# Selector matmuls and split latent projections: row copies by DMA and plain float32 matmuls in a two-layer trunk

## The chip, the cores and the metric

The kernel runs on one core of a Trainium2 chip. The metric is the device time of one execution in microseconds (us). The kernel before takes 2700.78 us, the median of 3 runs (2699.51 to 2701.32). A core has five engines that run at the same time, each with its own queue in program order: TensorE (PE, matmuls; its weight loads are shown as PEld), VectorE (DVE), ScalarE (ACT), GpSimd (POOL) and SyncE (SP), which here issues all transfers. Matmul results land in PSUM (8 banks of 128 x 512 float32), everything else lives in SBUF or in DRAM.

## The reference

Two layers on x of 1024 tokens by 1024 features, float32. Each layer normalizes x, multiplies by `w_in` (1024 x 9180), runs three branches (sparse attention over latent keys, stick-breaking attention, mLSTM), gates and projects them, and adds the result to x. What the change touches:

```python
# sparse attention: keys and values of all 8 heads come from one latent of rank 128
q_abs = jnp.einsum('bshn,rhn->bshr', q_nope, w_uk)
kv_cat = jnp.concatenate([c_kv, k_rope], axis=-1)      # 16 rotary features beside the latent
logits = jnp.einsum('bthf,btkf->bthk', qb, kv_sel)
o = jnp.einsum('bshr,rhv->bshv', o_lat, w_uv)
# mLSTM, 4 heads of 128, per chunk of tokens
w_intra = jnp.exp(log_d - m_row[..., None])            # log_d = b_t - b_s + i_s
w_inter = jnp.exp(log_inter - m_row)
num = s @ v + w_inter[..., None] * (q @ c_mem)
c_mem = decay[..., None, None] * c_mem + sum_s(w_upd * k * v)
```

The kernel uses the equal form in which keys `w_uk.T @ c_kv` (48 features a head, 16 rotary ones beside them) and values are built once for each pair of heads, and mLSTM chunks of 128 tokens.

## The kernel before

`body` writes a log of operations for the five engines in a natural order. `Plan.run` then places them: it plays the log with a table of costs (`cost`), takes on each engine the ready operation of lowest priority number, gives out SBUF and PSUM slots, and so fixes one order for each engine, which `emit` writes down. A change of an operation or of a cost can therefore move instructions anywhere. One line of `emit` writes every instruction, so all rows of the profile have the line L533, and views are told apart by shapes, tiles and time.

Large products run in "float32r", a one-pass float32 with shortened inputs: each operand is split into a high and a low part, and `PASSES` adds three products (high-high, high-low, low-high). The attention phases and the mLSTM are interleaved with background work: the top-k search (`tick`) and the gates of the branches (`AHEAD`), whose matmuls the planner takes when nothing else is ready.

Names that the change touches:

- `selm(j)` is a column of `sel_ml` repeated 128 times. A matmul with it as stationary operand copies row j of the moving operand (high part plus low part) to all 128 partitions of PSUM. In the mLSTM the log decays `rr_` and the factors `wi` (32 rows, one for each chunk and head, of 128 tokens) are split, written to DRAM (`pkd`), read back as 16 rows (`pk`), and for each head `h` and half `th` of the tokens copied by `selm(h)` (decays) and `selm(4 + h)` (factors). A bfloat16 matmul of `identb` with `m_ml` adds the causal mask to the copied decays in PSUM. 16 more selector matmuls of 4 columns (8 a layer) fetch the chunks' last factors (`dec`).
- `dsa_k(pr)` builds the keys of a head pair: three float32r matmuls of 512 columns for each half, and a fourth with `sel_kr` that adds the rotary rows (`krs`) below both heads. `stack_k` copies the result into two tiles (high part of one head over low part of the other).
- `dsa_v(pr)` builds values: for each of 8 token blocks three float32r matmuls of 256 columns.
- Plain float32 matmuls are there already: in the mLSTM the scores (`cv`, 128 columns) and the products of 129 columns with `Wt`, `qs`, `kw`.

Of the kernel before, what the change touches and what calls it, by code (L numbers as in the profile page):

```python
# [126 lines left out]
def cost(eng, meth, args, kw, ins, outs):  # L127
    n = max(free_size(a) for a in ins + outs)
    if eng == "PE":
        if meth == "transpose":  # L130
            return 109.5
        c = free_size(ins[1])
        dt = ins[1].tensor.dtype
        if dt == F32:
            return 2 * max(c * 0.4445, 109.0) + 2.5
        return max(c * 0.4445, 107.0 if dt == F32R else 36.0) + 4.0
# [477 lines left out]
def body(log, tiles, caps, x_in, w_in, w_uk, w_uv, kvn, conv_w, ib, fb, mln, w_br, w_out, nrm, fnrm,  # L614
# [50 lines left out]
    sel_kr = const([128, 128], F32R, "sel_kr")  # L665
    zer = const([128, 48], F32, "zer")
    V.memset(zer, 0.0)
    for e in range(2):
        V.tensor_tensor(sel_kr[:, 64 * e:64 * e + 16], ident[:, 0:16], ident[:, 16:32], ALU.add)
        V.tensor_copy(sel_kr[:, 64 * e + 16:64 * e + 64], zer)  # L670
    sel_ml = const([128, 8], F32R, "sel_ml")
    for j in range(8):
        k = (j % 4) + 8 * (j // 4)
        V.tensor_tensor(sel_ml[:, j:j + 1], ident[:, k:k + 1], ident[:, k + 4:k + 5], ALU.add)
# [10 lines left out]

    def selm(j):
        return sel_ml[:, j:j + 1].to_broadcast([128, 128])
# [109 lines left out]
    for l in range(DEPTH):  # L797
# [317 lines left out]
        hl = half(F32R)  # L1115
        pkd = dram([4, 32, 128], F32R)
        for q, src in ((0, rr_), (2, wi)):
            split(src, hl[0:32, q * 128:q * 128 + 128], hl[0:32, q * 128 + 128:q * 128 + 256])
        for q in range(4):
            SY.dma_start(f(pkd[q]), f(hl[0:32, q * 128:q * 128 + 128]))  # L1120
        pk = []
        for th in range(2):
            k = half(F32R)
            pk.append(k)
            G.memset(f(k[:, :512]), 0.0)
            for q in range(4):
                SY.dma_start(f(k[4 * q:4 * q + 4, :512]).rearrange("h (c t) -> h c t", c=4),
                             f(pkd[q, 16 * th:16 * th + 16, :]).rearrange("(c h) t -> h c t", h=4))
# [5 lines left out]
        pd = pst("tr")  # L1134
        for h in range(4):
            for th in range(2):
                PE.matmul(pd[:, h * 8 + th * 4:h * 8 + th * 4 + 4], selm(4 + h),
                          pk[th][:, 127:512:128], start=True, stop=True)
        dec = small([128, 4, 8], name="dec", bufs=1)
# [615 lines left out]
```

## Time and profile before

| | |
|---|---|
| median of 3 runs | 2700.78 us |
| profiled execution | 2701.0 us |
| its span, first to last instruction | 2699.2 us |
| busy: PE, PEld | 2660.6 us (99%), 2245.6 us (83%) |
| busy: DVE, ACT, POOL | 1753.4 us (65%), 1484.8 us (55%), 1086.3 us (40%) |
| matmul records | 14802 |
| granted TensorE clock | 0.998 of full speed |

"Busy" of PE is the union of the records' durations. Matmuls overlap, so a record of 128x512 lasts 394 ns while the next one starts earlier; the rate is read from a stretch that holds one shape only: (busy time minus one duration) over (count minus one). The profile writes float32r and float32 both as "f32". The layers run one after the other; phases of a layer in order are the first projections and the scores of the top-k search (to about 100 us in layer 0), the mLSTM (to about 450 us), stick-breaking attention (to about 760 us), sparse attention (to about 1100 us), gates and output product (to about 1343 us). Layer 1 repeats this from there.

### The profile page before, as it was taken

What the parts mean: (1) busy time and instruction counts of PE and PEld (TensorE: products, weight loads), DVE (VectorE), ACT (ScalarE), POOL (GpSimd) and SP (SyncE); (2) the same over time, 40 slices, a digit from 0 to 9 for tenths busy, and PEclk for the clock granted to TensorE, in tenths of its full rate; (3) what the DMA queues carried; (4) which work ended last, traced back from release to release, by engine and by line L of the source; (5) the groups of instructions that cost most, each with busy time, mean ns of one, the idle gap of its engine ahead of it and who ended that gap; (6) DMA issues with size and microseconds to landing.
All of it is one profiled execution on the core that took longest, in us unless ns stands there. A gap on an engine that the chain in (4) does not pass through costs nothing.

```text
span 2699.2 us, 42025 instructions
## 1 busy us (share of the span) xinstructions
PE 2660.6 (99%) x14802; PEld 2245.6 (83%) x14802; DVE 1753.4 (65%) x4076; ACT 1484.8 (55%) x3004; POOL 1086.3 (40%) x1433
## 2 busy tenths in 40 slices
PE   8999999999999999999999999999999999999998
PEld 7888878888888888888898888888888888888886
DVE  5828789667586653426867287986676766634277
ACT  4637773545466857611446368735555677675023
POOL 4323334233253524444725143342342444244536
PEclk9999999999999999999999999999999999999999
DMA  4302112112122214664204021222121322256531
GB/s 132 99 16 65 54 55 72 51 55 80 36 88 68 78 55 141 224 222 152 76 25 120 14 79 52 63 67 59 36 75 44 96 59 71 62 179 230 180 117 63
DMA packets 234632, 236.86 MB, mean 88 GB/s; under 512 B 22250, under 2 KB 181300, under 8 KB 234420
## 3 DMA queue, kind: packets, MB, share of 16 engines
q1 hardware_dynamic: 234420, 234.17, 27.5%
q8 instruction: 117, 1.92, 0.3%
q14 instruction: 95, 0.78, 0.1%
HBM read 171.78 MB, written 62.32 MB: 87 GB/s over the span
## 4 chain that ended last, share of the span: by engine, by line
PE 51%; ACT 4%; DVE 2%; issue 1%; DMA 1%; POOL 0%; SPq 0%; DVEq 0%; ACTq 0%; POOLq 0%
PE t L533 51%; ACT t L533 3%; DVE t L533 2%; ACT s L533 1%; DMA t<-in_w_in_dram 1%; ACT L533 1%; POOL t L533 0%; DVE s L533 0%; SPq L533 0%; DMA d<-t 0%; DVEq L1751 0%; ACTq L533 0%; DVEq L533 0%; POOLq L533 0%
## 5 line engine op out<-in xcount | busy, mean ns | idle before, releaser
L533 PE MATMUL t<-t,t 128*128 128x512 f32 (+5 forms) x14094 | 2536.7, 342 | 27.8 <-DVE t L533 22.2
L533 PEld LDWEIGHTS t<-t,t 128*128 128x128 f32 x13950 | 2114.0, 183 | 397.6 <-DVE t L533 36.2
L533 POOL TENSOR_TENSOR t<-t,t 128x256 fp32r<-128x256 f32 (+3 forms) x946 | 754.3, 825 | 1074.3 <-ACT t L533 446.0
L533 DVE TENSOR_TENSOR t<-t,t 128x512 f32<-128x512 f32 (+15 forms) x1514 | 761.6, 534 | 592.7 <-ACT t L533 489.0
L533 ACT CAST t<-t 128x512 fp32r<-128x512 f32 (+6 forms) x1047 | 532.6, 551 | 473.3 <-PE t L533 240.7
L533 ACT ACTIVATE t<-t 128x512 f32<-128x512 f32 (+5 forms) x699 | 346.9, 592 | 266.4 <-PE t L533 196.5
L533 ACT ACTIVATE t<-t,t 128x768 bf16<-128x768 f32 (+7 forms) x343 | 273.6, 817 | 25.7 <-DVE t L533 19.6
L533 ACT COPY t<-t 64x256 f32<-64x256 f32 (+4 forms) x296 | 110.2, 380 | 257.2 <-PE t L533 254.9
L533 DVE TENSOR_TENSOR_SCAN t<-t 128x256 f32<-128x256 f32 (+10 forms) x144 | 209.3, 1463 | 7.1 <-ACT t L533 6.7
L533 DVE SCALAR_TENSOR_TENSOR t<-t,t,t 128x512 f32<-128x512 f32 (+7 forms) x220 | 166.7, 781 | 12.5 <-POOL t L533 5.3
L533 POOL TENSOR_SCALAR t<-t 64x512 fp32r<-64x512 f32 x128 | 85.2, 666 | 198.9 <-ACT t L533 145.3
L533 ACT ACT_TABLE_LOAD x114 | 146.3, 1283 | 23.7 <-PE t L533 14.5
L533 POOL TENSOR_SCALAR t<-t,t 128x256 f32<-128x256 f32 (+7 forms) x128 | 95.3, 753 | 134.1 <-DVE t L533 126.3
L533 DVE TENSOR_TENSOR s<-s,t 128x512 f32<-128x512 f32 (+1 forms) x93 | 67.4, 728 | 106.4 <-PE t L533 103.7
L533 DVE TENSOR_SCALAR_CACHE_REDUCE t<-t,t 128x512 bf16<-128x512 f32 (+5 forms) x169 | 125.7, 770 | 1.0
L533 PE MATMUL t<-s,t 128*128 128x512 f32 (+1 forms) x336 | 112.4, 386 | 0.0
L533 DVE CUSTOM_DVE_ANT_0 t<-t,t 128x512 f32<-128x512 f32 (+3 forms) x160 | 92.6, 592 | 21.3 <-PE t L533 18.7
L533 PEld LDWEIGHTS t<-s,t 128*128 128x128 f32 x336 | 62.0, 188 | 13.8
L533 DVE TENSOR_SCALAR t<-t 128x1 f32<-128x1 f32 (+5 forms) x324 | 58.0, 187 | 9.1 <-ACT t L533 6.5
L533 PE MATMUL t<-t,s 128*128 128x512 f32 (+1 forms) x200 | 63.3, 389 | 0.0
L533 DVE RECIPROCAL t<-t 128x1 f32<-128x1 f32 (+1 forms) x144 | 23.0, 163 | 61.2 <-ACT t L533 60.2
L533 DVE TENSOR_TENSOR t<-t 128x1 f32<-128x1 f32 (+9 forms) x234 | 54.4, 244 | 4.1 <-POOL t L533 1.6
(54 smaller groups left out, 823.4 us busy)
## 6 DMA issues: line engine op xcount, KB each, us to landing
t<-in_w_in_dram SPq DMA_DIRECT2D x192, 256.0 KB
d<-t SPq DMA_DIRECT2D x134, 256.0 KB
t<-d SPq DMA_DIRECT2D x119, 256.0 KB
t<-in_w_in_dram SPq DMA_DIRECT2D x44, 512.0 KB
s<-d SPq DMA_DIRECT2D x85, 256.0 KB
d<-t SPq DMA_DIRECT2D x130, 128.0 KB
t<-in_w_branch_dram SPq DMA_DIRECT2D x24, 512.0 KB
t<-in_x_dram SPq DMA_DIRECT2D x16, 512.0 KB
```

Source lines behind the costliest of these rows:

```text
L533: fn(*args, **kw)
```

## The change

The decays and factors of the mLSTM go to DRAM unsplit (`row_d`), and for each head and half one transfer with a partition step of zero copies the row to all 128 partitions of an SBUF tile (`row`). The mask is added to the decays by GpSimd. The chunk's last factor is read as a column of the same tile. In sparse attention the latent is kept unsplit, keys and values take one plain float32 matmul each, and the rotary rows are written into the finished key tiles by four small transfers for each half. The selector tiles go. The planner's price of a plain float32 matmul in `cost` changes.

```diff
         if dt == F32:
-            return 2 * max(c * 0.4445, 109.0) + 2.5
+            return 2 * max(c * 0.83 + 3.5, 109.0) + 2.5
...
-        hl = half(F32R)
-        pkd = dram([4, 32, 128], F32R)
-        for q, src in ((0, rr_), (2, wi)):
-            split(src, hl[0:32, q * 128:q * 128 + 128], hl[0:32, q * 128 + 128:q * 128 + 256])
-        for q in range(4):
-            SY.dma_start(f(pkd[q]), f(hl[0:32, q * 128:q * 128 + 128]))
-        pk = []
-        for th in range(2):
-            k = half(F32R)
-            pk.append(k)
-            G.memset(f(k[:, :512]), 0.0)
-            for q in range(4):
-                SY.dma_start(f(k[4 * q:4 * q + 4, :512]).rearrange("h (c t) -> h c t", c=4),
-                             f(pkd[q, 16 * th:16 * th + 16, :]).rearrange("(c h) t -> h c t", h=4))
+        row_d = dram([2, 32, 128])
+        for q, src in enumerate((rr_, wi)):
+            SY.dma_start(row_d[q], src)
+
+        def row(q, h, th):
+
+            r = half()
+            a = row_d[q, 16 * th + h:16 * th + h + 1, :]
+            SY.dma_start(r[:, :512].rearrange("p (c t) -> p c t", c=4),
+                         bass.AP(tensor=a.tensor, offset=a.offset, ap=[[0, 128], [512, 4], [1, 128]]))
+            return r
...
-        pd = pst("tr")
-        for h in range(4):
-            for th in range(2):
-                PE.matmul(pd[:, h * 8 + th * 4:h * 8 + th * 4 + 4], selm(4 + h),
-                          pk[th][:, 127:512:128], start=True, stop=True)
...
+            rows_ = []
+            for th in range(2):
+                r = row(0, h, th)
+                pool_tt(r, r, m_ml.rearrange("p a b -> p (a b)"), ALU.add, 512)
+                rows_.append((r, row(1, h, th)))
             tick(2)
             for th in range(2):
-                p = pst("lg")
-                PE.matmul(p, selm(h), pk[th][:, :512], start=True, stop=False)
-                PE.matmul(p, identb, m_ml.rearrange("p a b -> p (a b)"), start=False, stop=True)
+                rrow, wrow = rows_[th]
                 Wt = half()
                 for t in range(4):
                     c = th * 4 + t
-                    S.activation(Wt[:, t * 128:t * 128 + 128], p[:, t * 128:t * 128 + 128], AF.Exp,
+                    S.activation(Wt[:, t * 128:t * 128 + 128], rrow[:, t * 128:t * 128 + 128], AF.Exp,
                                  bias=mlc[:, 0, c, h:h + 1])
...
-                p = pst("lg")
-                PE.matmul(p, selm(4 + h), pk[th][:, :512], start=True, stop=True)
                 qs = half()
-                V.tensor_tensor(qs[:, :512], cv[0, th][:, :512], p, ALU.mult)
+                V.tensor_tensor(qs[:, :512], cv[0, th][:, :512], wrow[:, :512], ALU.mult)
...
-                            V.scalar_tensor_tensor(Cn, Cst, dec[:, h, c:c + 1], p[:, :129], ALU.mult, ALU.add)
+                            V.scalar_tensor_tensor(Cn, Cst, wrow[:, t * 128 + 127:t * 128 + 128], p[:, :129],
+                                                   ALU.mult, ALU.add)
...
         for th in range(2):
             c = half()
             SY.dma_start(c[:, :512], ckvT_d[:, th * 512:th * 512 + 512])
-            hi, lo = pair(F32R)
-            split(c[:, :512], hi, lo)
...
-            k = half(F32R)
-            G.memset(f(k[:, :512]), 0.0)
-            for q in range(2):
-                SY.dma_start(f(k[16 * q:16 * q + 16, :512]), f(kr_d[q, :, th * 512:th * 512 + 512]))
-            krs.append(k)
+            ck.append(c)
...
-            uw = half(F32R)
-            S.copy(uw[:, 0:128], us[:, :128])
-            G.tensor_tensor(uw[:, 128:256], us[:, :128], f(uw[:, 0:128]), ALU.subtract)
             r = dict(k=[], q=[None, None], z=[None, None])
             for th in range(2):
                 p = pst("mm")
-                for i, (a, b) in enumerate(PASSES):
-                    PE.matmul(p, uw[:, 128 * a:128 * a + 128], ck[b][th][:, :512], start=(i == 0), stop=False)
-                PE.matmul(p, sel_kr, krs[th][:, :512], start=False, stop=True)
-                r["k"].append(stack_k(p))
+                PE.matmul(p, us[:, :128], ck[th][:, :512], start=True, stop=True)
+                k = stack_k(p)
+                for e in range(2):
+                    for q in range(2):
+                        o = 64 * (e ^ q)
+                        SY.dma_start(f(k[e][o:o + 16, :512]), f(kr_d[q, :, th * 512:th * 512 + 512]))
+                r["k"].append(k)
...
-                    for i, (a, b) in enumerate(PASSES):
-                        PE.matmul(p[:, t * 256:t * 256 + 256],
-                                  ck[b][sb // 4][:, (sb % 4) * 128:(sb % 4) * 128 + 128],
-                                  uw[:, 256 * a:256 * a + 256], start=(i == 0), stop=(i == 2))
+                    PE.matmul(p[:, t * 256:t * 256 + 256], ck[sb // 4][:, (sb % 4) * 128:(sb % 4) * 128 + 128],
+                              us[:, :256], start=True, stop=True)
```

What the planner makes of it is shown in three places. The rows below are an engine's instructions in order: operation, output tile, inputs (for a matmul the moving and then the stationary one), shape; buffers have numbers of their own in each kernel. The first place is PE at the first head of the mLSTM, layer 0, before. `t_2286` takes `selm(0)` (`t_114`, moving `pk` as `t_1377`) and the mask, `t_2302` takes `selm(4)`.

```order
L533 MATMUL t_2270<-t_93,t_1708 128x128 x4
L533 MATMUL t_2277<-t_93,t_1755 128x128 x4
L533 MATMUL t_2286<-t_1377,t_114 128x512
L533 LDWEIGHTS t_97
L533 MATMUL t_2286<-t_103,t_97 128x512
L533 MATMUL t_2292<-t_1607,t_1708 128x128 x4
L533 MATMUL t_2302<-t_1377,t_114 128x512
L533 MATMUL t_2304<-t_1790,t_2283 128x129
L533 MATMUL t_2308<-t_1790,t_2283 128x129
```

The same place now, from the same transposes (`t_2240`, `t_2248`) on:

```order
L533 MATMUL t_2240<-t_92,t_1670 128x128 x4
L533 MATMUL t_2248<-t_92,t_1742 128x128 x4
L533 MATMUL t_2258<-t_1578,t_1670 128x128 x4
L533 MATMUL t_2267<-t_1771,t_2256 128x129
L533 MATMUL t_2269<-t_1771,t_2256 128x129
L533 MATMUL t_2273<-t_1833,t_2256 128x129
L533 MATMUL t_2278<-t_1833,t_2256 128x129
L533 MATMUL t_1432<-t_218,t_1282 128x512
L533 MATMUL t_2283<-t_1630,t_1742 128x128 x3
L533 MATMUL t_2291<-t_1771,s_1934 128x129
```

The three 512-column matmuls are gone, and four products with `kw` (`t_2256`) have come forward to stand between the scores (`t_2258`) and the first product with `Wt` (`s_1934`). The second place is PE at the first keys and values of sparse attention, layer 0, before: `t_9193` and `t_9202` are the keys of the two halves (the last matmul of each with `sel_kr`, `t_87`), the four tiles of 256 columns are the values.

```order
L533 MATMUL t_9193<-t_8369,t_8826 128x512 x3
L533 MATMUL t_9193<-t_8315,t_87 128x512
L533 MATMUL t_9202<-t_8406,t_8826 128x512 x3
L533 MATMUL t_9202<-t_8317,t_87 128x512
L533 MATMUL t_9213<-t_8871,t_8369 128x256 x6
L533 MATMUL t_9224<-t_8871,t_8369 128x256 x6
L533 MATMUL t_9234<-t_8871,t_8406 128x256 x6
L533 MATMUL t_9245<-t_8871,t_8406 128x256 x6
L533 MATMUL t_9257<-t_93,t_8844 128x128 x4
```

The same place now; `t_9138` is a key tile made from `t_9129`, and the last row shown is the first that reads it.

```order
L533 MATMUL t_9129<-t_8297,t_8672 128x512
L533 MATMUL t_9135<-t_8303,t_8672 128x512
L533 MATMUL t_9142<-t_8712,t_8297 128x256 x2
L533 MATMUL t_9152<-t_8712,t_8297 128x256 x2
L533 MATMUL t_9160<-t_8712,t_8303 128x256 x2
L533 MATMUL t_9170<-t_8712,t_8303 128x256 x2
L533 MATMUL t_9179<-t_92,t_8828 128x128 x4
L533 MATMUL t_9187<-t_212,t_8869 128x512
...
L533 MATMUL t_9187<-t_259,t_8918 128x512
L533 MATMUL t_9235<-t_9138,t_9197 128x128
```

Eight matmuls of 512 columns have become two, and 24 of 256 have become eight; behind them stand, as before, four transposes and the 24 matmuls of a gate (`t_9187`, two of which are shown) until the first logits. The third place is SP, where transfers are issued, at the start of the mLSTM of layer 0, before (`d_1586` is `pkd`, `t_1377` and `t_1379` are `pk`):

```order
L533 DMA d_1586<-t_1580 32x128 x3
L533 DMA t_1605<-in_w_in_dram 128x4x256
L533 DMA d_1586<-t_1580 32x128
L533 DMA t_1377<-d_1586 4x4x128 x3
L533 DMA t_1379<-d_1586 4x4x128 x3
L533 DMA t_1377<-d_1586 4x4x128
L533 DMA t_1379<-d_1586 4x4x128
L533 DMA t_1649<-in_w_in_dram 128x4x256
```

and now (`d_1560` is `row_d`; the tiles it is read into are the rows of head 0, and the two `s` tiles at the end those of head 1):

```order
L533 DMA d_1560<-t_1548 32x128 x2
L533 DMA t_1638<-in_w_in_dram 128x4x256
L533 DMA t_1823<-d_1560 128x4x128
L533 DMA t_1829<-d_1560 128x4x128
L533 DMA t_1838<-d_1560 128x4x128
L533 DMA s_1859<-d_1560 128x4x128
L533 DMA t_1968<-in_w_in_dram 128x4x128
L533 DMA t_1979<-in_w_in_dram 128x4x128
L533 DMA t_1968<-in_w_in_dram 128x4x128
L533 DMA t_1979<-in_w_in_dram 128x4x128
L533 DMA s_2182<-d_1560 128x4x128 x2
L533 DMA s_2205<-d_1560 128x4x128 x2
```

Eight small reads at the start have become four transfers of 256 KB for each head, which stand between the weight loads.

## Rows read from the trace of the kernel before

**Rows 1.** The page: span, busy time by engine, granted TensorE clock in 40 slices.
```profile
span 2699.2 us, 42025 instructions
PE 2660.6 (99%) x14802; PEld 2245.6 (83%) x14802; DVE 1753.4 (65%) x4076; ACT 1484.8 (55%) x3004; POOL 1086.3 (40%) x1433
PEclk9999999999999999999999999999999999999999
```

**Rows 2.** Waits of PE, whole span: us in total, times, longest.
```profile
PE t L533 <- DVE t L533: 22.2, 20, 7.9
PE t L533 <- ACT t L533: 1.9, 6, 0.4
PE t L533 <- POOL t L533: 1.0, 4, 0.5
```

**Rows 3.** Groups by shape on PE, 1495 to 1538 us: xcount | busy, mean ns.
```profile
L533 PE MATMUL t<-t,t 128*128 128x512 f32 x187 | 43.5, 394 | 0.0
```

**Rows 4.** The same on PE, 1772 to 1792 us.
```profile
L533 PE MATMUL t<-t,t 128*128 128x256 f32 x172 | 20.4, 280 | 0.0
```

**Rows 5.** The same on PE, 211.2 to 212.35 us (a run of plain float32 matmuls).
```profile
L533 PE MATMUL t<-t,t 128*128 128x129 f32 x11 | 1.4, 275 | 0.0
```

**Rows 6.** The same on PE, 128.58 to 129.24 us (the decays' selector matmuls).
```profile
L533 PE MATMUL t<-t,t 128*128 128x4 f32 x7 | 0.8, 239 | 0.0
```

**Rows 7.** Groups by shape on PE, whole span.
```profile
L533 PE MATMUL t<-t,t 128*128 128x129 f32 x344 | 56.6, 283 | 6.5 <-DVE t L533 5.9
L533 PE MATMUL t<-t,t 128*128 128x512 bf16 x16 | 6.2, 390 | 0.0
L533 PE MATMUL t<-t,t 128*128 128x4 f32 x16 | 2.0, 230 | 0.0
L533 PE MATMUL t<-t,s 128*128 128x129 f32 x8 | 1.4, 274 | 0.0
```

**Rows 8.** Groups by shape on POOL, whole span: additions of 256 columns.
```profile
L533 POOL TENSOR_TENSOR t<-t,t 128x256 f32<-128x256 f32 x32 | 22.9, 738 | 134.3 <-DVE t L533 134.3
```

**Rows 9.** Busy time of each engine in the mLSTM and sparse attention phases.
```profile
core 0: us, PE busy (x) PEld busy (x) DVE busy (x) ACT busy (x) POOL busy (x), PEclk, DMA share, GB/s
195.00:450.00 255.00, 249.72 (x1410) 214.71 (x1409) 212.12 (x562) 172.21 (x335) 94.79 (x126) 0.99 0.20 59
1480.00:1760.00 280.00, 277.56 (x1502) 234.13 (x1500) 194.15 (x518) 183.19 (x350) 97.59 (x138) 1.00 0.18 53
760.00:1100.00 340.00, 337.68 (x2013) 285.85 (x2012) 203.14 (x583) 232.68 (x480) 144.61 (x209) 1.00 0.30 92
2050.00:2440.00 390.00, 385.78 (x2305) 326.34 (x2304) 252.20 (x672) 277.83 (x579) 156.29 (x225) 1.00 0.29 88
```

**Rows 10.** The page: DMA queue, packets, MB, share of 16 engines' span.
```profile
q1 hardware_dynamic: 234420, 234.17, 27.5%
```

**Rows 11.** Timeline of SP, 121 to 127 us: start, us, xcount.
```profile
121.81 3.71 SPq L533 DMA_DIRECT2D t<-d  x8
125.57 1.49 SPq L533 DMA_DIRECT2D t<-in_w_in_dram  x3
```

**Rows 12.** Timeline around PE's longest wait after the start: start, us, [idle before].
```profile
346.48 1.88 DVE L533 TENSOR_TENSOR t<-t,t 128x512 f32<-128x512 f32 x3
347.23 1.17 PE L533 MATMUL t<-t,t 128*128 128x129 f32 x3 [3.95 <-DVE t L533]
```

**Rows 13.** The chain that ended last, 2096 to 2106 us: start, us, what.
```profile
2097.01 0.34 SPq L533
...
2097.44 6.23 DMA t<-in_w_in_dram
...
2103.70 1.05 ACT t L533
...
2105.17 0.43 DVE t L533
```

**Rows 14.** Groups by shape on ACT and DVE, whole span: the copies of `stack_k` and `stack_q`.
```profile
L533 ACT CAST t<-t 64x512 fp32r<-64x512 f32 x128 | 74.9, 587 | 60.8 <-PE t L533 36.8 <-DVE t L533 22.2
L533 DVE TENSOR_TENSOR t<-t,t 64x512 fp32r<-64x512 f32 x128 | 92.2, 721 | 55.8 <-ACT t L533 52.4 <-POOL t L533 1.6
```

More of the change, by code (lines that the diff above doesn't have):

```diff
@@ L664, in body @@
     V.memset(neghalf, -0.5)
[L665 to L674, printed above, removed]
     tk_thr = const([128, 6], F32, "tk_thr")
@@ L684, in body @@
             V.memset(tk_sign[:, i:i + 1], -0x80000000)
-    def selm(j):
-        return sel_ml[:, j:j + 1].to_broadcast([128, 128])
     def bcast(ap, n):
@@ L1133, in body @@
         V.tensor_copy(mlc.rearrange("p q c h -> p (q c h)"), p[:, 0:96])
-        pd = pst("tr")
-        for h in range(4):
-            for th in range(2):
-                PE.matmul(pd[:, h * 8 + th * 4:h * 8 + th * 4 + 4], selm(4 + h),
-                          pk[th][:, 127:512:128], start=True, stop=True)
-        dec = small([128, 4, 8], name="dec", bufs=1)
-        V.tensor_copy(dec, pd[:, 0:32].rearrange("p (h c) -> p h c", h=4))
         SCL = 128.0 ** -0.5
@@ L1432, in body @@
             return
-        ckh, ckl = [], []
-        krs = []
+        ck = []
         for th in range(2):
@@ L1439, in body @@
             SY.dma_start(c[:, :512], ckvT_d[:, th * 512:th * 512 + 512])
-            hi, lo = pair(F32R)
-            split(c[:, :512], hi, lo)
-            ckh.append(hi)
-            ckl.append(lo)
-            k = half(F32R)
-            G.memset(f(k[:, :512]), 0.0)
-            for q in range(2):
-                SY.dma_start(f(k[16 * q:16 * q + 16, :512]), f(kr_d[q, :, th * 512:th * 512 + 512]))
-            krs.append(k)
-        ck = (ckh, ckl)
+            ck.append(c)
         def dsa_q(gq):
@@ L1484, in dsa_v @@
             SY.dma_start(us[:, :256], w_uv[l, :, 2 * pr:2 * pr + 4, :].rearrange("r h c -> r (h c)"))
-            uw = half(F32R)
-            S.copy(uw[:, 0:256], us[:, :256])
-            G.tensor_tensor(uw[:, 256:512], us[:, :256], f(uw[:, 0:256]), ALU.subtract)
             vs = [[], []]
```

## The prediction

> **What bounds the kernel now.** I read the page first: PE is busy for 2660.6 of 2699.2 us, the other engines for 65% or less, and the granted clock stands at full speed in every slice [rows 1]. The waits of PE come next: 22.2, 1.9 and 1.0 us for DVE, ACT and POOL, 25.1 together, of which the longest, 7.9, is the start [rows 2]. So beyond the start only some 17 us of the span are waits of PE that a new order could remove, and nearly everything else is matmuls one behind the other. The third view is the rate of each shape. In stretches with one shape only, 512 columns of float32r take (43.5 - 0.394)/186 = 0.232 us each [rows 3], 256 columns (20.4 - 0.28)/171 = 0.118 us [rows 4]. A plain float32 matmul leaves two records: the mLSTM has 22 products of 129 columns for each of 8 heads, 176 in all, and the trace holds 344 + 8 = 352 [rows 7]. A record of these takes (1.4 - 0.275)/10 = 0.112 us [rows 5]. In all four phases that the change touches PE is busy for 98 to 99% of the stretch [rows 9]. A matmul taken away there is therefore time taken away, unless a new wait fills the place.
>
> **The mLSTM's matmuls.** For each of 2 layers, 4 heads and 2 halves three matmuls of 512 columns go: two selectors and the mask. The mask's is bfloat16; its 390 ns [rows 7] are those of a float32r one (394), so I price it alike. 16 x 3 x 0.232 = 11.1 us go. The decays' 16 selector matmuls of 4 columns [rows 7] take (0.8 - 0.239)/6 = 0.09 us, some 0.1 [rows 6]: 1.6 us go. Together -12.7 us, all on PE.
>
> **The latent products.** Keys: 2 layers x 4 pairs x 2 halves = 16 times, four matmuls of 512 columns (4 x 0.232 = 0.927) become one plain one. Values: 2 layers x 2 calls x 8 blocks = 32 times, three of 256 (3 x 0.118 = 0.353) become one plain one. The trace has no plain matmul wider than 129 columns, so I bound it. At least, each of its two records costs as much as a float32r matmul of that width: 0.464 and 0.235 us; then the keys give 16 x 0.463 = 7.4 and the values 32 x 0.118 = 3.8 us. At most, each record costs two of them: 0.927 and 0.471; then the keys give nothing and the values lose 32 x 0.118 = 3.8 us. The nearest row is the plain product of 129 columns: 0.112/129 = 0.868 ns a column and record, nearly twice the 0.232/512 = 0.453 of float32r. At this narrow width 0.112 could also be a floor that has nothing to do with columns (the selector matmuls of 4 columns take almost as much [rows 6]), which is why the lower end stays. I take the row: 512 columns cost 2 x 0.444 = 0.889, 256 cost 0.444. Keys: 16 x (0.889 - 0.927) = -0.6 us. Values: 32 x (0.444 - 0.353) = +2.9 us. So this half of the change loses 2.3 us by my reading, with ends at -11.2 and +3.8.
>
> The Trainium skill has a rule that speaks against this half: the page "FP8 and Floating Point Precision", section "TensorE Precision Notes", says that a true float32 product takes four passes through the array. By it a plain matmul costs four float32r ones, 0.927 and 0.471, the keys are even, the values lose 3.8 us, and the whole sum would be -8.9 us. The two records for each product fit two passes in each; no row here shows a width at which passes could be counted.
>
> **What the copies cost elsewhere.** The rows' mask goes to POOL: 16 rows x 2 pieces x 0.738 [rows 8] = 23.6 us of POOL, which is busy for 95 of 255 and 98 of 280 us in the mLSTM [rows 9]. That hides it as long as it comes before the exponentials. 32 transfers of 256 KB are 8.4 MB; 234 MB take 27.5% of 16 engines' span [rows 10], so these take 1.0% more, in phases where the engines are used to 0.18 and 0.20. SP issues a read in 3.71/8 = 0.46 and a weight load of the rows' shape in about 0.50 us [rows 11]: 32 x 0.50 + 64 x 0.46 for the rotary rows, less 0.46 for each of some 32 small ones that go, +31 us of a queue that issues some 930 transfers in 2700 us. ACT reads the decays from SBUF where it read PSUM, the same 128-column exponentials; the `qs` product on DVE has both inputs in SBUF. Splits on ACT, DVE and POOL go. None of this is on PE; I put it at nothing, covered by PE's own stream, and at up to the rivals' prices if that cover is gone.
>
> **The added waits.** A key tile is read only when its rotary rows have landed. The tightest place is the first pair, where the order of the change has behind the first key matmul one more key matmul (0.89), eight of 256 columns (3.6), four transposes (0.1 each, by the floor above) and the gate's 24 matmuls (5.6 us) before the first logits: 10.5 us. In this time come two copies on ACT and two on DVE, 2 x (0.587 + 0.721) = 2.6 us [rows 14], four issues, 1.9, and a landing, at most the 6.2 that weight loads took in a busy stretch [rows 13]: 10.7 us at worst. I take no wait there. Behind the rotary transfers on SP stand mask and weight loads and the stores of finished heads, which is a rival's matter below.
>
> **The sum.** -12.7 - 0.6 + 2.9 = -10.4 us. The profiled execution took 2701.0 (span 2699.2 and 1.8 around it), 0.2 above the median of 2700.78. 2701.0 - 10.4 = 2690.6, against the median 2690.4; I say 2690. For comparison: a measurement tells a change from none at about 0.2%, 5.4 us here.
>
> **Rival 1: plain matmuls are no slower than one float32r record each.** Then the sum is -12.7 - 11.2 = -23.9 us, 2677. For it speaks only that the 0.112 us of [rows 5] could be a floor; against it, weakly since both are read from short runs, that a selector of 4 columns, with less to stream, comes out below 0.112 [rows 6].
>
> **Rival 2: the new order eats the gain.** The planner places everything anew, and small misjudgements come out elsewhere. Before, PE's waits beyond the start sum to 17 us, one of them 3.95 us behind a late DVE product [rows 12]. Two or three more of that size give back 8 to 12 us: 2698 to 2702, no change. Against it: the same 17 us can also shrink, the mLSTM has one PSUM product and its wait less in every half, and the order around the three places shown is otherwise the one of before. If the waits shrink by half instead, 2682.
>
> **Rival 3: SP's queue holds the weights up, and the kernel is slower.** SP issues in order. At 2097 us a store waited for ACT; two weight loads behind it landed 6.23 us later, and through ACT (1.05) and DVE (0.43) their lateness reached PE [rows 13]. The change puts eight transfers that wait for `stack_k` into this queue at each of 8 pairs, and four row transfers that wait for free tiles at each of 8 heads. If each of these 16 places makes PE wait for about 2 us, the kernel is at -10.4 + 32 = +22 us, 2722. It decides from (10.4 + 5.4)/16 = 1.0 us for each place. Against it: all of PE's waits beyond the start are 17 us, this chain's among them, and the places lie far apart: by [rows 9] a head of the mLSTM spans some 255/4 = 64 us and a pair some 340/4 = 85, in which weights can be loaded ahead.
>
> **Rival 4: POOL's additions hold DVE in the mLSTM.** DVE is busy there for 212 of 255 and 194 of 280 us [rows 9], PE's waits are nearly all for DVE [rows 2], and additions of 23.6 us could delay DVE by as much, in the worst case all of it passed on: -10.4 + 23.6 = +13, 2714. The point is a delay on PE of 15.8 us, two thirds of the additions' whole time; since DVE has 43 and 86 us to spare there, I hold this unlikely. The Trainium skill, "SBUF — State Buffer", section "SBUF: two separate sides", says that a GpSimd operation and a VectorE one with both inputs in SBUF lock each other out for a whole instruction. The rows here show no instruction of either kind alone and beside the other, so the rule stands unproved in this case.
>
> **Chances.** The forecast, 2684 to 2697: 0.62. Rival 1: 0.07. The waits shrink, below 2684: 0.04. Rival 2, within 5.4 us of before: 0.15. Rival 3: 0.08. Rival 4: 0.04. Faster by over 0.2%: 0.62 + 0.07 + 0.04, less 0.01 for the forecast's upper edge: 0.72; within: 0.15 + 0.01 = 0.16; slower: 0.12. The range goes from rival 1's 2677 to 2703, just over rival 2's waits; outside it lie rivals 3 and 4 and little else.
>
> **What will show it.** In the profile after, PE's records should be 14802 - 48 - 16 - 16 x (4 - 2) - 32 x (3 - 2) = 14674, its busy time some 10 us less, with the waits of PE near 25 us. In runs of the key and value products a record should take about 0.44 us at 512 columns and 0.22 at 256: 0.23 and 0.12 would mean rival 1. The mLSTM stretches should be shorter by about 6 us in each layer, sparse attention longer by about 1. PE waits for DVE above 35 us in the mLSTM would speak for rival 4, waits of ACT for weight loads with PE behind them for rival 3, and scattered new ones for rival 2. The forecast is wrong if the records are gone and the span is not about 10 us shorter.

## The result

The changed kernel takes 2676.78 us (median of 4 runs, 2673.4 to 2679.29) against 2701.05 for the kernel before beside it: a ratio of 0.9912, interval 0.99 to 0.9923, 24 us faster. The forecast was 2690 with a range of 2677 to 2703, so the direction was right, the gain was more than twice the 10.4 us of the sum, and the time lies just below the range.

The page after, first lines, against [rows 1]:

```profile
span 2675.3 us, 41890 instructions
PE 2641.5 (99%) x14674; PEld 2234.8 (84%) x14674; DVE 1745.4 (65%) x4053; ACT 1480.8 (55%) x2986; POOL 1110.6 (42%) x1445
```

The 14674 records are those forecast. PE's busy time fell by 19.1 us and the span by 23.9, where both were to fall by about 10. PE's waits after (who is waited for: us, times, longest), against [rows 2]:

```profile
PE t L533 <- DVE t L533: 16.3, 14, 8.0
PE t L533 <- ACT t L533: 3.7, 3, 2.6
PE t L533 <- POOL t L533: 2.4, 6, 0.8
```

They sum to 22.4 us, 2.7 less than before. So the view of waits shows little of the 14 us that came on top of the forecast; most of it is inside PE's busy time, because a record lasts longer than the step to the next one.

To see it, I priced every record in program order at its shape's rate in a pure run (us for each record: float32r of 512, 256, 384, 220, 128 columns 0.232, 0.118, 0.176, 0.111, 0.061; plain of 512, 256 and 128 or 129 columns 0.429, 0.216, 0.1115; transposes 0.109; bfloat16 of 512 and 128 columns 0.232 and 0.039; the few others 0.11). Their sum I call **work**. The time from the first to the last start of a record, less the work, I call **slack**: the waits of the view and all small delays together, worked out by me from the records and shown by no view. From first to last start it is 2680.2 us before and 2657.0 after. Work is 2591.0 and 2579.5 (-11.5), slack 89.3 and 77.7 (-11.6). The work came out about as forecast; the slack had been put at no change.

Where the slack went, by the phase of the record that came late, both layers together: mLSTM 15.1 to 7.9, gates in the background 7.1 to 2.3, sparse attention 31.4 to 31.1, stick-breaking attention 24.5 to 24.1, first projections 3.3 to 4.6, the start 7.8 and 7.9.

**The plain products.** The weight loads of PE in the changed kernel, 2132.5 to 2138.1 us, show their rate (start, us, xcount, [idle before]); the loads before 2134.54 belong to keys of 512 columns, 16 of the group of 17 behind them to values of 256:

```profile
2133.26 0.19 PEld L533 LDWEIGHTS t<-t,t 128*128 128x128 f32 x1 [0.24 <-issue]
2133.68 0.19 PEld L533 LDWEIGHTS t<-t,t 128*128 128x128 f32 x1 [0.24 <-issue]
2134.11 0.19 PEld L533 LDWEIGHTS t<-t,t 128*128 128x128 f32 x1 [0.24 <-issue]
2134.54 3.60 PEld L533 LDWEIGHTS t<-t,t 128*128 128x128 f32 x17 [0.24 <-issue]
```

A record of 512 columns takes 0.43 us (2134.54 - 2134.11), one of 256 about (3.60 - 0.19)/16 = 0.213, a little low because the last load of the group is a shorter one; the matmuls' own starts give 0.429 and 0.216. Forecast were 0.444 and 0.222; rival 1 needed 0.23 and 0.12.

**The mLSTM's products of 129 columns.** Groups by shape on PE in the changed kernel (xcount | busy, mean ns | idle before them), against the 6.5 us idle in [rows 7]:

```profile
L533 PE MATMUL t<-t,t 128*128 128x129 f32 x264 | 43.9, 277 | 2.0 <-DVE t L533 1.9
L533 PE MATMUL t<-t,s 128*128 128x129 f32 x88 | 14.4, 274 | 0.0
```

The wait of 3.95 us [rows 12] has gone.

### The profile page after: what moved, and what is told of

It is laid out like the page before. It is cut to its first block, busy times and chain, and to the rows that moved or that the text cites. A ratio compares the mean times of both kernels' runs of the same rounds, so it can differ in the third digit from the quotient of the medians.

```text
span 2675.3 us, 41890 instructions
## 1 busy us (share of the span) xinstructions
PE 2641.5 (99%) x14674; PEld 2234.8 (84%) x14674; DVE 1745.4 (65%) x4053; ACT 1480.8 (55%) x2986; POOL 1110.6 (42%) x1445
## 4 chain that ended last, share of the span: by engine, by line
PE 89%; ACT 4%; DVE 3%; issue 2%; DMA 1%; POOL 1%; SPq 0%; POOLq 0%; ACTq 0%; DVEq 0%
PE t L533 89%; ACT t L533 3%; DVE t L533 3%; DMA t<-in_w_in_dram 1%; ACT L533 1%; POOL t L533 1%; DMA t<-in_x_dram 0%; ACT s L533 0%; DMA d<-t 0%; SPq L533 0%; DVE s L533 0%; POOLq L1716 0%; ACTq L533 0%; POOLq L533 0%; DVEq L533 0%
## 5 line engine op out<-in xcount | busy, mean ns | idle before, releaser
L533 PE MATMUL t<-t,t 128*128 128x512 f32 (+6 forms) x13826 | 2503.9, 343 | 23.9 <-DVE t L533 16.3
L533 POOL TENSOR_TENSOR t<-t,t 128x256 fp32r<-128x256 f32 (+4 forms) x956 | 772.0, 836 | 1016.9 <-ACT t L533 433.5
L533 DVE TENSOR_TENSOR t<-t,t 128x256 fp32r<-128x256 f32 (+12 forms) x1492 | 744.9, 528 | 588.0 <-ACT t L533 479.7
L533 ACT CAST t<-t 128x512 fp32r<-128x512 f32 (+5 forms) x1030 | 525.9, 552 | 489.9 <-PE t L533 260.8
L533 ACT ACTIVATE t<-t 128x512 f32<-128x512 f32 (+5 forms) x700 | 347.6, 587 | 262.2 <-PE t L533 200.5
L533 ACT ACTIVATE t<-t,t 128x1024 bf16<-128x1024 f32 (+9 forms) x320 | 288.8, 906 | 36.0 <-DVE t L533 30.0
L533 DVE SCALAR_TENSOR_TENSOR t<-t,t,t 128x512 f32<-128x512 f32 (+9 forms) x202 | 162.2, 826 | 10.4 <-POOL t L533 6.3
L533 ACT ACT_TABLE_LOAD x116 | 148.8, 1283 | 14.7 <-PE t L533 10.5
L533 POOL TENSOR_SCALAR t<-t,t 128x128 f32<-128x128 f32 (+7 forms) x128 | 95.7, 756 | 131.1 <-DVE t L533 126.0
L533 POOL TENSOR_TENSOR t<-s,s 128x256 fp32r<-128x256 f32 x52 | 53.4, 1052 | 53.8 <-issue 28.7
L533 DVE TENSOR_SCALAR t<-t 128x1 f32<-128x1 f32 (+6 forms) x324 | 59.7, 193 | 9.1 <-ACT t L533 6.8
L533 PE MATMUL t<-s,s 128*128 128x512 f32 x192 | 63.0, 394 | 0.0
```

Source lines behind the costliest of these rows:

```text
L533: fn(*args, **kw)
```

## The experiments

All ratios stand against the kernel before, run beside them on the same chip; it took 2699.36 to 2701.05 us there. Work, slack and the mLSTM's part of the slack are worked out from the trace of each, and each trace is one order of the operations. In the traces of `before_x1`, `before_x3`, `lat_x1`, `lat_x3`, `kr_only`, `plain_only` and `before_junk` 8 matmul records are missing; they are priced with the rest:

| kernel | time, us | ratio, interval | work | slack | mLSTM |
|---|---|---|---|---|---|
| before | 2700.78 | | 2591.0 | 89.3 | 15.1 |
| before_cost | 2701.62 | 1.0003 (0.9994-1.0013) | 2591.0 | 90.4 | 16.5 |
| before_x1 | 2707.93 | 1.0031 (1.0019-1.0042) | 2591.0 | 95.9 | 20.6 |
| before_x3 | 2707.02 | 1.0026 (1.0015-1.0037) | 2591.0 | 92.9 | 19.1 |
| ml_only | 2679.41 | 0.9925 (0.9909-0.9942) | 2578.1 | 78.8 | 7.0 |
| lat_only | 2691.65 | 0.997 (0.9958-0.9982) | 2592.4 | 77.6 | 16.1 |
| lat_x1 | 2689.83 | 0.9961 (0.9941-0.998) | 2592.4 | 77.9 | 14.2 |
| lat_x3 | 2695.01 | 0.9978 (0.9967-0.9989) | 2592.4 | 84.8 | 15.2 |
| kr_only | 2698.04 | 0.9993 (0.9983-1.0003) | 2587.3 | 91.9 | 18.2 |
| plain_only | 2696.88 | 0.999 (0.998-1.0001) | 2596.1 | 81.2 | 15.3 |
| after | 2676.78 | 0.9912 (0.99-0.9923) | 2579.5 | 77.7 | 7.9 |
| after_oldcost | 2675.96 | 0.9911 (0.9896-0.9925) | 2579.5 | 77.0 | 7.5 |
| split_lat | 2677.66 | 0.9916 (0.9902-0.9931) | 2574.4 | 81.9 | 7.4 |
| sel_dec | 2676.03 | 0.991 (0.9895-0.9925) | 2586.9 | 69.7 | 8.4 |
| sel_fac | 2677.63 | 0.9917 (0.9902-0.9932) | 2585.0 | 71.4 | 6.1 |
| idle_mm | 2687.42 | 0.9955 (0.9939-0.9972) | 2590.6 | 76.1 | 10.4 |
| before_junk | 2694.25 | 0.998 (0.9971-0.9989) | 2591.0 | 82.2 | 3.8 |
| after_junk | 2669.77 | 0.9889 (0.9873-0.9906) | 2579.5 | 66.9 | 2.1 |
| after_junk_x1 | 2667.80 | 0.9879 (0.9863-0.9895) | 2579.5 | 67.7 | 1.9 |
| splitl_junk | 2676.11 | 0.9912 (0.9897-0.9927) | 2574.4 | 80.8 | 2.5 |

My first theory, A, was that a copy by PE heads a chain PE, ACT, DVE, PE, and that this chain's waits go with it. Its rival, B, was luck of the new order.

### The halves alone, and the price line alone

The mLSTM's part of the diff alone (`ml_only`) and the latent part alone (`lat_only`), both with the new price; the price line alone (`before_cost`); and the whole change with the old price (`after_oldcost`):

```diff
-            return 2 * max(c * 0.4445, 109.0) + 2.5
+            return 2 * max(c * 0.83 + 3.5, 109.0) + 2.5
```

> The mLSTM half of the change alone (rows by transfers, mask on GpSimd; latent keys and values as before), with the new price of plain matmuls. It takes 16 x 3 matmuls of 0.232 us and 16 of 0.1 off PE: -12.7 us of work. Theory A (the copies by PE stood at the head of a chain PE, ACT, DVE, PE, and the waits for it went with them): the mLSTM's waits fall by some 7 us too, about -20 us, 2681. Theory B (the waits fell by luck of the new order): anything between -6 and -20, with the waits in the mLSTM not systematically lower.

> The latent half alone, with the new price. By the trace of the changed kernel a plain matmul takes 2 x 0.429 us at 512 columns and 2 x 0.216 at 256, so keys save 16 x (0.927 - 0.858) = 1.1 and values lose 32 x (0.432 - 0.353) = 2.5: +1.4 us of PE work. Theory A: about 2702, the mLSTM's waits as before. Theory B: 2695 to 2708 by the order. A price of one float32r record each would give -11 us, 2690.

> The kernel before with only the planner's new price of plain matmuls (for 128 and 129 columns 222 and 224 ns in place of 220): the same work on every engine, another order. Theory A: 2701 within 4 us. Theory B: the time moves by 5 us or more, since the order alone is worth that.

> The changed kernel with the planner's old price of plain matmuls: the same work as the changed kernel, another order. Theory A: 2677 within 4 us. Theory B: it loses much of the 12 us that the work does not explain, 2683 to 2690.

The price line reorders PE and is worth nothing on either side. The mLSTM half brings 20 us alone: 12.9 of work and 10.5 of slack, 8 of it in the mLSTM, as A wants. The latent half was a miss: its work rises by 1.4 us, yet it is 8 us faster, with 12 us less slack and none of that in the mLSTM. Together the halves take away 12 us of slack, not 22: the gains do not add.

### Other orders of the same work

`EXTRA` is added to the delay, in ns, that the planner assumes between an instruction and one on another engine that needs it (so it is not a rule for matmuls alone, as the expectations put it). Another number reorders everything and leaves the work alone (1.0 in `before_x1` and `lat_x1`, 3.0 in `before_x3` and `lat_x3`):

```diff
-EXTRA = 0.0
+EXTRA = 1.0
```

> The kernel before with another number in the planner's rule for leaving room ahead of a matmul (1.0): the same work, another order; nothing is left out. Its matmuls are worth 2591.0 us at the rates of the pure stretches and before had 89.3 us of waits beside them, 15.1 in the mLSTM. If the waits belong to the structure of the program (A): again 86 to 93 us of waits, some 15 in the mLSTM, time 2698 to 2705. If they are luck of the order (B): the waits scatter by the 12 us that the change won, so 77 to 100 us here, 2689 to 2712, and the mLSTM's part can be 8 as well as 20.

> As the run with 1.0, with 3.0 instead: the same work as before in a third order. A: waits of 86 to 93 us, mLSTM some 15, time 2698 to 2705. B: anywhere in 2689 to 2712.

> The latent half of the change alone, with the same other number in the planner's rule (1.0): another order of the work of the kernel whose time was 2691.65 us with 77.6 us of waits. Its matmuls are worth 2592.4 us. If this half takes waits away by its structure (fewer steps between a load and the first matmul): waits of 75 to 81 us again, time 2689 to 2695, the mLSTM's waits unchanged at 15 to 16. If its 12 us were luck of one order: waits back at 84 to 92, 2698 to 2706, in this run or the next.

> The latent half alone in a third order (3.0). By structure: 75 to 81 us of waits, 2689 to 2695. By luck: 84 to 92, 2698 to 2706, here or in the run with 1.0.

Orders scatter by some 7 us within a family, more than A allowed: before had 89 to 96 us of slack, and in two orders is 7 to 8 us slower. `lat_x3` is a partial miss: its 84.8 us of slack fall into the branch of luck, its 2695.01 us at the edge of the other. But four orders of before (89.3 to 95.9) and three of the latent half (77.6 to 84.8) do not overlap, nor do the two orders of the whole change (77.0 and 77.7), so B alone does not explain the gain. The mLSTM's slack is 14 to 21 in all seven.

### Which of the latent half's parts

`kr_only` brings the rotary rows by transfers and keeps the float32r passes; `plain_only` makes the products plain and keeps `sel_kr`:

```diff
-                    PE.matmul(p, uw[:, 128 * a:128 * a + 128], ck[b][th][:, :512], start=(i == 0), stop=False)
+                PE.matmul(p, us[:, :128], ck[th][:, :512], start=True, stop=False)
                 PE.matmul(p, sel_kr, krs[th][:, :512], start=False, stop=True)
```

> The kernel before with the rotary rows by transfers alone; latent keys and values stay three float32r products, the mLSTM as before. 16 matmuls of 512 columns go: 2591.0 - 3.7 = 2587.3 us of work. The family of before has 89 to 96 us of waits, that of the latent half 78 to 85. If the rotary rows' copies held the latent half's waits: 78 to 85 here, time 2685 to 2692. If the split products did: 89 to 96, 2696 to 2703.

> The kernel before with plain float32 products for latent keys and values alone; the rotary rows stay a selector matmul, added to the plain product. 16 x (0.859 + 0.232 - 0.927) + 32 x 0.079 = 5.1 us more work, 2596.1. If the splits and three passes held the waits: 78 to 85 us, time 2694 to 2701. If the rotary copies did: 89 to 96, 2705 to 2712.

Both came out as the split theory said: rows by transfers leave the slack at 91.9, plain products bring it to 81.2. So the plain products pay for 5.1 us more work with some 11 us of slack. By phase, part of it can be placed: among the kernels with the mLSTM's copies on PE, sparse attention has 30.2 to 33.7 us of slack and the gates 5.4 to 9.6 in the six orders that split the latent, 27.9 to 29.5 and 0.5 to 3.9 in the four that do not. Among the kernels with the mLSTM's rows by transfers these ranges overlap. `split_lat` asks the same of the changed kernel: it splits the latent again and has less work.

```diff
-                PE.matmul(p, us[:, :128], ck[th][:, :512], start=True, stop=True)
+                for i, (a, b) in enumerate(PASSES):
+                    PE.matmul(p, uw[:, 128 * a:128 * a + 128], ck[b][th][:, :512], start=(i == 0), stop=(i == 2))
```

> The kernel after, with the latent keys and values as three float32r products again; rows still come by transfers, no selector for the rotary keys. By the records of after a plain product of 512 columns costs 0.859 us and three float32r ones 3 x 0.232 = 0.696, of 256 columns 0.432 against 0.353: 16 x 0.163 + 32 x 0.079 = 5.1 us less work, 2574.3. With waits as in after (77.0 and 77.7 us in two orders): 2671.7, range 2668 to 2676, faster than both kernels. If the splitting of the latent tiles on ACT, DVE and POOL is what cost the waits that the latent half alone lost (12 us): some of them come back, 2677 to 2684.

The 5.1 us did not show: 81.9 us of slack, some 4 to 5 more than in the two orders of after, and the same time. This is one order, and 4 to 5 us lie within the scatter of orders. No one place holds the difference; sparse attention, stick-breaking attention and the gates differ by a few us each.

### Which copy of the mLSTM

`sel_dec` copies decays and mask by PE again, `sel_fac` the factors, `idle_mm` adds three matmuls that nothing reads in each half-head; the core of each in this order:

```diff
+                p = pst("lg")
+                PE.matmul(p, selm(h), pk[th][:, :512], start=True, stop=False)
+                PE.matmul(p, identb, m_ml.rearrange("p a b -> p (a b)"), start=False, stop=True)
```

```diff
+                PE.matmul(p, selm(h), pk[th][:, :512], start=True, stop=True)
-                V.tensor_tensor(qs[:, :512], cv[0, th][:, :512], wrow[:, :512], ALU.mult)
+                V.tensor_tensor(qs[:, :512], cv[0, th][:, :512], p, ALU.mult)
```

```diff
+                p = pst("lg")
+                for i in range(3):
+                    PE.matmul(p, sta(4 * th)(0, i), mov(0, i, th), start=(i == 0), stop=(i == 2))
```

> The kernel after, with the mLSTM's decays and mask by selector matmuls on PE again (16 x 2 of 512 columns, +7.4 us of work); the factors of the queries and of the state still come by transfers. If the chain PE, ACT (exponentials), DVE (times the scores), PE held the waits (A): the mLSTM's waits go from 7.9 back to 13 to 17 us, time 2677 + 7.4 + 5 to 9 = 2689 to 2693. If the factors' copy held them: the waits stay at 7 to 9, time 2684, range 2681 to 2687.

> The kernel after, with the factors of the queries and of the state by selector matmuls again (16 of 512 columns, 16 of 4: +3.7 + 1.4 = 5.1 us of work); the decays and the mask stay as in after. If the decays' chain held the waits (A): the mLSTM's waits stay at 7 to 9 us, time 2682, range 2679 to 2685. If the factors' copy held them (PE, DVE, PE): 13 to 17 us, time 2687 to 2691. If both have a part, about half of it in each of these two runs.

> The kernel after, with three idle matmuls of 512 columns into a PSUM tile of their own in each of the 16 half-heads of the mLSTM, where the copies stood; nothing reads them. 48 x 0.232 = 11.1 us of work. If the copies cost the time of their columns and the wait of what read them (A): the mLSTM's waits stay at 7 to 9 us, time 2688, range 2685 to 2691, so the waits do not come back with the matmuls. If it was the PSUM tile or the place on PE that cost the waits: the mLSTM's waits go to 13 to 20 us, time 2693 to 2699.

The idle matmuls cost 10.6 us (11.5 when each kernel is taken against the before run beside it), about their columns' price of 11.1; the mLSTM's slack of 10.4 us lies between the two branches. But A falls with the other two, which came out below both of their branches, 5 and 1.4 us under the lower one: putting one copy back adds 7.4 or 5.5 us of work to PE and no time at all, and the mLSTM's slack stays at 6 to 8 us whichever copy is back. So it is not a chain behind either copy. Idle time before the products of 129 columns in `before_x3`, `sel_dec` and `sel_fac` (larger group of each):

```profile
L533 PE MATMUL t<-t,t 128*128 128x129 f32 x352 | 56.8, 281 | 10.5 <-DVE t L533 10.1
```

```profile
L533 PE MATMUL t<-t,t 128*128 128x129 f32 x296 | 48.0, 278 | 0.4
```

```profile
L533 PE MATMUL t<-t,t 128*128 128x129 f32 x288 | 48.0, 276 | 0.2
```

### What DVE did before PE's wait

The next place is DVE ahead of the wait of [rows 12]. DVE in the kernel before, 343.3 to 347.6 us (start, us, [idle before <-who ended it]); buffers named `s` are the large ones that small tiles share when their own run out:

```profile
343.33 0.74 DVE L533 TENSOR_SCALAR_CACHE_REDUCE s<-t,t 128x512 bf16<-128x512 f32 x1
343.99 0.09 DVE L533 DVE_READ_ACCUMULATOR s<-t,t 128x1 f32 x1
345.68 0.88 DVE L533 TENSOR_SCALAR_CACHE_REDUCE s<-t,t 128x640 bf16<-128x640 f32 x1 [1.60 <-ACT s L533]
346.48 0.09 DVE L533 DVE_READ_ACCUMULATOR s<-t,t 128x1 f32 x1
346.48 1.28 DVE L533 TENSOR_TENSOR t<-t,t 128x512 f32<-128x512 f32 x2
```

And ACT in the same stretch:

```profile
344.51 1.04 ACT L533 ACTIVATE s<-t,t 128x896 bf16<-128x896 f32 x1
345.46 0.19 ACT L533 ACTIVATION_READ_ACCUMULATOR s<-t,t 128x1 f32 x1
```

This is a counting round of the top-k search, work of another branch: it compares scores with a threshold and keeps only the sums; the compared values go into a buffer (`junk`) that nobody reads. DVE's third count uses no result of ACT, but in the program its output is placed in the other half of the large buffer into which ACT counts 896, and it waits until that count ends at 345.65. Behind it in DVE's order stand the copies `kw`, for which PE waits until 347.23. The same rows with the same 1.60 us stand at 1691 us in `before_x3`, and PE's wait behind them:

```profile
1690.76 0.88 DVE L533 TENSOR_SCALAR_CACHE_REDUCE s<-t,t 128x640 bf16<-128x640 f32 x1 [1.60 <-ACT s L533]
```

```profile
1692.31 0.49 PE L533 MATMUL t<-t,t 128*128 128x129 f32 x2 [3.94 <-DVE t L533]
```

The wait costs more than its own time. Three stretches of PE in the kernel before (us, PE busy (x), PEclk, DMA share, GB/s):

```profile
343.20:347.20 4.00, 0.08 (x1) 0.98 0.00 0
347.20:350.70 3.50, 3.48 (x12) 0.53 0.00 0
350.70:354.20 3.50, 3.50 (x25) 1.00 0.00 0
```

After the wait the granted clock is 0.53, nearly the lower of its two levels (1.2 in place of 2.4 GHz), and PE starts 12 matmuls where the next 3.5 us hold 25. The 40 slices of [rows 1], 67 us each, do not show it. Eight kernels with the mLSTM's copies on PE (before, `before_cost`, `before_x1`, `before_x3`, `lat_only`, `lat_x3`, `kr_only`, `plain_only`) have 11 such waits of 2.9 to 4.4 us there, each followed by a stretch at the lower level that costs 1.6 to 3.4 us more by the prices above. Taken together, waits and stretches are 5.9 us of the 15.1 of before; without theirs, all eight have some 6 to 10 us of slack in the mLSTM, about what the changed kernel has, where no such wait is left. `lat_x1` has none either and still 14.2, so this is not the whole.

In the changed kernel the copies come before the round: DVE at 338 us, with the next count at 341.84.

```profile
338.13 0.85 DVE L533 TENSOR_TENSOR t<-t,t 128x512 f32<-128x512 f32 x2
...
341.84 0.60 DVE L533 TENSOR_SCALAR_CACHE_REDUCE t<-t,t 128x384 bf16<-128x384 f32 x1
```

### Buffers of their own for the counting rounds

One such buffer for ACT and one for DVE, and two shared ones fewer; no matmul changes:

```diff
-N_HALF = 21
+N_HALF = 19
...
-                junk = half(BF16, 1040)
+                junk = small([128, 1040], BF16, name="jka" if i in TK_ACT else "jkv", bufs=1)
```

> The kernel before, with two buffers set apart for the counting rounds' unused outputs (one for ACT, one for DVE) and two fewer shared ones; the same matmuls, 2591.0 us. If the wait of DVE for a buffer that ACT still counts into is what holds the third head's state update (theory J): DVE's waits of 1.6 us are gone in the mLSTM, PE's waits of 4 us at 347 too, the mLSTM's waits fall from 15-20 to 7-10 us, time 2691 to 2696. If it is the place of the rounds in DVE's order, ahead of the copies that the state update reads (theory P): the waits stay at 13 to 20 us, time 2698 to 2707.

> The kernel after with the same two buffers set apart. The mLSTM has only 8 us of waits left. J: DVE's waits for ACT's buffers go here too, but PE hardly waits behind them: time 2673 to 2678, waits of 74 to 79 us in all. P: the same within the scatter of orders, 2673 to 2682.

> The kernel after with the rounds' own buffers, with the other number (1.0) in the planner's rule: the same work in another order. If the gain of 7 us is the buffers': 2667 to 2674, waits of 65 to 72 us, the mLSTM's 1 to 4. If it was luck of that order: 2674 to 2680, waits of 73 to 79.

> The kernel after with buffers of their own for the counting rounds (its time was 2669.77 us, 66.9 us of waits) and with the latent keys and values as three float32r products again: 5.1 us less work, 2574.4. If the splits cost waits only through the buffers that the rounds then lack: waits of 65 to 70 us, time 2665, range 2662 to 2668, the fastest yet. If the splits cost waits in any case: waits of 72 to 78, time 2670 to 2676, no better than with the plain products.

DVE's waits for ACT's shared buffers over the whole span, `before` and `after`; all of the first and 7.8 us of the second stand before counts:

```profile
DVE s L533 <- ACT s L533: 12.3, 11, 1.6
```

```profile
DVE s L533 <- ACT s L533: 8.6, 10, 1.6
```

The larger part are the counts of 640 columns, `before` and `before_junk` (xcount | busy, mean ns | idle before them); in `before_junk` no count waits for ACT:

```profile
L533 DVE TENSOR_SCALAR_CACHE_REDUCE s<-t,t 128x640 bf16<-128x640 f32 x12 | 10.6, 880 | 9.7 <-ACT s L533 9.5
```

```profile
L533 DVE TENSOR_SCALAR_CACHE_REDUCE t<-t,t 128x640 bf16<-128x640 f32 x66 | 57.8, 876 | 1.5
```

Another wait stays: the comparison of 6 columns that ends a round needs ACT's counts themselves. DVE's idle time there grows, `before` and `before_junk`:

```profile
L533 DVE TENSOR_TENSOR t<-t,t 128x6 f32<-128x6 f32 x64 | 15.3, 239 | 42.2 <-ACT t L533 30.7 <-ACT s L533 11.4
```

```profile
L533 DVE TENSOR_TENSOR t<-t,t 128x6 f32<-128x6 f32 x64 | 16.1, 252 | 67.9 <-ACT t L533 67.7
```

So DVE's waiting as such need not cost time; it does where PE needs what stands behind it in DVE's order. In `sel_dec` DVE's waits for ACT's shared buffers are 11.2 us by the same view as above, nearly those of before, and the mLSTM's slack is 8.4.

In `before_junk` PE does not wait at the products of 129 columns, and DVE waits for PE in front of the `kw` copies:

```profile
L533 PE MATMUL t<-t,t 128*128 128x129 f32 x324 | 47.4, 275 | 0.0
```

```profile
345.28 0.69 DVE L533 TENSOR_TENSOR t<-t,t 128x512 f32<-128x512 f32 x1 [5.96 <-PE t L533]
```

The clock at the same place stays up:

```profile
347.20:350.70 3.50, 3.50 (x29) 1.00 0.00 0
```

The mLSTM's slack falls from 15.1 to 3.8 us with both copies still on PE, where four orders of before have 15.1 to 20.6; the whole slack falls by 7.1, so some 4 us appear elsewhere. The kernel before gains 0.2% (interval 0.11 to 0.29%), 5 us, in the one order that was tried, which is less than the scatter of orders, and 13 to 14 us against `before_x1` and `before_x3`. The changed kernel gains as well, and more than either J or P said: 2669.77 and, in the second order, 2667.80, whose interval (0.9863 to 0.9895) lies below the one of after (0.99 to 0.9923). These are the fastest kernels of the study. Since the rounds are moved along with their buffers, what is shown is that the shared buffers, with the order that they force, hold the wait; the one without the other was not tried. The buffer's own 1.60 us are less than half of PE's 3.95. PE's waits in `after_junk`, the start of 7.9 among them:

```profile
PE t L533 <- DVE t L533: 13.0, 9, 7.9
PE t L533 <- POOL t L533: 1.6, 4, 0.5
PE t L533 <- ACT t L533: 0.7, 3, 0.2
```

`splitl_junk` missed both branches of its expectation on the slow side: split again, it has 13 to 14 us more slack than the two orders of `after_junk` (80.8 against 66.9 and 67.7), 7 to 9 of them in sparse attention, and is 6 to 8 us slower with 5 us less work. It is one order, but the difference is larger than the scatter. So the splits cost slack with the rounds' own buffers too.

## Why the prediction was wrong

- **mLSTM, -12.7:** right as work. The records that went are worth 12.9 us, and `idle_mm` charges 10.6 us for 48 such matmuls. That a matmul taken away is time taken away did not hold one for one: `sel_dec` and `sel_fac` take 7.4 and 5.5 us of them back and lose no time.
- **Keys -0.6, values +2.9:** right in kind and size, -1.1 and +2.5 by the records' 0.429 and 0.216 us: 16 x (0.859 - 0.927), and 32 x (0.432 - 0.353). A plain product costs 0.859/0.232 = 3.7 float32r ones of its width. The Trainium skill, "FP8 and Floating Point Precision", section "TensorE Precision Notes", says four passes; four at the price of a float32r matmul would be 0.928 us, an estimate above what the trace has. Whether a pass costs as much as a float32r matmul, no run shows.
- **Rival 1** gave 2677, nearly the time, and is refuted: the plain products are not cheap. A time alone does not choose between mechanisms.
- **"Nearly everything else is matmuls one behind the other":** this is the step that failed. From PE busy for 98 to 99% and 25 us of waits I took it that only some 17 us could move with the order. The work is 2591.0 of 2680.2 us; 89 us are slack, 64 of them hidden in records that overlap the next. How much of it could go is not shown, but in the 20 kernels here it ranges from 66.9 to 95.9, 29 us. I used the pure rates for what was taken away and never summed them over what stayed.
- **"I put it at nothing":** the removed splits and copies, with the new order, were not worth nothing: -11.6 us of slack. In the mLSTM it is PE's wait of 3.95 us and the lower clock behind it, 5.9 of the 7.2 us lost there; the wait hangs on where the counting rounds stand and which buffers they share (`before_junk`). Why the change moves them out of the way is not shown. In the latent half it was slack that comes with the split products, some 11 us beside the mLSTM's copies, 4 beside its rows, 13 to 14 with the rounds' own buffers (shown by `kr_only`, `plain_only`, `split_lat`, `splitl_junk`). Its mechanism stays open, as does why the two gains do not add and why taking back one copy of the mLSTM costs no time.
- **The case "the waits shrink by half", 2682,** had 0.04 and the right sign, but is not what happened: the waits of the view beyond the start shrank by about 3 of 17 us, and the slack that the view does not list by 9. Rival 2 gave the order's changes the other sign; `before_x1` and `before_x3` show that it can go there too, by 7 to 8 us.
- **Against rival 1** the prediction read 0.09 us for a selector matmul of 4 columns from [rows 6]. Six of the seven records there start 0.111 to 0.112 us apart; the other is a short one that the next follows after 0.03. So they cost what a plain product of 129 columns does, that argument falls, and a floor could not be excluded. That the price by columns held at 256 and 512 was in part luck.
- **Rivals 3 and 4** did not appear. POOL is busy 24.3 us longer (forecast 23.6), PE's waits for it rose from 1.0 to 2.4. No wait of PE for a transfer is listed in after, though transfers grew from [rows 10] to:

```profile
q1 hardware_dynamic: 252596, 244.20, 29.2%
```

That is 10.0 MB, and 1.7% of the engines' span where 1.0 was forecast for 8.4 MB; the bytes of the rotary rows' small transfers were not priced.

## What to carry to other kernels

Before forecasting an edit to a kernel whose matmul engine is 99% busy, price all its records at pure-run rates: what is left over bounds what the order can move, and here it was three and a half times what the view of waits lists. Where PE waits for DVE, read what stands before the awaited instruction in DVE's order and what that waited for; here it was a side job's output that nobody reads, and two buffers of its own, with the order that came with them, were worth 5 us in one kernel (one order) and 7 to 9 in the other (two orders). Run two or three reorders that change no work before giving a reason for less than their scatter, here 7 us.

## What was not expected of the hardware

A wait of PE of 2.9 to 4.4 us in the mLSTM was followed by a granted clock of about half, which cost 1.6 to 3.4 us more; the page's slices showed full speed throughout. The plain float32 matmul costs nearly the same for each record and column at three widths: 0.112 us/129 = 0.87 ns, 0.216/256 = 0.84 and 0.429/512 = 0.84. The wide ones show a rate; at 129 columns, where a selector of 4 columns takes the same 0.11 us, rate and floor cannot be told apart. Idle matmuls cost 10.6/48 = 0.22 us each, about as much as useful ones in a pure run (0.232), and their PSUM tiles brought little back: the mLSTM's slack rose by 2.5 us.
